# Front of a one-layer hybrid block: the first memory keys by plain fp32 products, and the loads in another order

## The chip, the core and the metric

The kernel runs on one core of a Trainium2 chip. The metric is device time in microseconds (us) of one execution. The core has a matrix engine (TensorE, "PE" in the profile, with its weight loads as "PEld"), a vector engine (VectorE, "DVE"), a scalar engine (ScalarE, "ACT"), GpSimd ("POOL") and SyncE ("SP"), which here only issues transfers. Each engine takes its instructions in order. Transfers from the chip's large memory are issued by SP, ACT or POOL; those of one issuer stand in one queue, and all share 16 DMA engines.

## The reference, cut to what matters

A layer works on 512 frames of 1024 channels (`x`) and on 256 memory tokens of 1024 channels (`mem`), in float32. `x` and `mem` are normalised, three branches attend, their gated sum goes through an output product, and a squared-ReLU MLP follows. This case concerns the first steps only:

```
u = rmsnorm(h, g_mix)                              # h = x at the start
mkv = rmsnorm(mem, g_mem) @ w_mem_kv               # 256 x 1024
mk, mv = split(mkv)                                # memory keys and values, 512 columns each
proj = u @ w_in                                    # every projection of the layer starts from u
```

The row factor of `rmsnorm(mem, g_mem)` is one number per memory token, so the kernel multiplies by `g_mem` first, forms the products, and applies that number later.

## The kernel before, in words

**Products in parts.** A float32 product is made of three fast products. Each operand is split: ACT casts it to the fast format (the high part, `hi`), DVE subtracts that from the original (the low part, `lo`). `mm3` (lines 154 to 157) then adds high by high, high by low and low by high into the same accumulator. Weights come as chunks of 128 partitions by 1024 numbers (512 KB); `chunk_list` gives their order. Chunks 0 to 3 are the four key blocks, 4 to 7 the values, 8 is a small gate chunk ("G"), and from 9 on come the projections of `u`.

**The front** (lines 251 to 363) runs once and before everything else. Its parts:

- Twelve products of zeros (line 279) keep TensorE busy until data arrive. A memset on GpSimd (line 276) makes their operand.
- ACT's queue brings the memory tokens in four pieces (`memr`, line 282). SP's queue brings the gains `cols`, then chunk 0 in quarters, chunk 1, two small pieces of the constants (`ident` and `ones`, 128 KB; `mhalf`, 4 KB), chunks 2 and 3, the four tiles of `x` (`xn`, line 300, 512 KB each), chunk 4, and the other constants (lines 302 to 304). `lead` (lines 258 to 269) issues such a chunk and splits it.
- ACT and DVE make the parts `mxh`, `mxl` of the memory tokens times `g_mem` (lines 288 and 289), one eighth at a time.
- Four key blocks (`mk_proj`) are 24 products of 128x256 each. For each contraction step `gT` issues all three products of `mm3`, so the low part of the weights is needed at the third product.
- `x_norm(t)` makes one tile of `x` ready: a sum of squares on ACT (line 327), two small steps on DVE and GpSimd (lines 214 and 215, the latter a power with `mhalf`), a scaling on DVE (line 329).
- `u_turn(k)` transposes one block of 128 channels of all four tiles on TensorE with the identity (line 341); ACT and DVE split the result into `uhi` and `ulo` (lines 342 and 343). The eight transposed blocks are taken in turn with the four value chunks: two blocks, one chunk (12 products of 128x512 for two token tiles), two blocks, one chunk, and so on. Here the second product already needs the low part of the weights.
- `g_proj` (lines 410 to 420) then projects `u` with chunk G, and the layer goes on with chunks 9, 10 and so forth.

**What sets the order.** TensorE's order is the order in which the code is written. The order on the other engines is planned: a simulated run at build time places each instruction by the time at which it is ready there; `issue_after` ties one instruction behind another. Buffers for raw chunks, high and low parts (`raw`, `hi`, `lo`) exist three times each; two more raw ones (`lead`) serve chunks 3 and 4. Four accumulator banks are for keys and projections, four for values and transposes. Each chunk split by `split_w` also counts towards `next_sum`, which from the twelfth on issues one weight-sum transfer per chunk on GpSimd's queue for the MLP.

The step that is split for the vector engine, as the front uses it:

```
raw, hi, lo = (t[:, sl] for t in pre[key])
nc.sync.dma_start(raw, wst[index[key]][:, sl])
cast = nc.scalar.copy(hi, raw).ins
nc.vector.tensor_tensor(lo, raw, f(hi), op=ALU.subtract)
```

Of the kernel before, what the change touches and what calls it, by code (L numbers as in the profile page):

```python
# [9 lines left out]
F32 = mybir.dt.float32  # L10
# [7 lines left out]
P = 128  # L18
# [46 lines left out]
def hybrid_block(ctx, tc, chunks, wst, memT, xN, cols, gffn, gfin, wup, cst, out):  # L65
# [26 lines left out]
        return ap.bitcast(F32)  # L92


    cst_s = cp.tile([P, 7 * P + 8], F32, name="cst_s")
    cols_s = cp.tile([P, 24], F32, name="cols_s")
    msk_s = cp.tile([P, 2, P], U8, name="msk_s")
    wup_s = cp.tile([P, 264], F32, name="wup_s")
    ident, ones, tri, mids = (cst_s[:, i * P:(i + 1) * P] for i in range(4))
    mhalf = cst_s[:, 6 * P:6 * P + 8]  # L100
    cmask = cst_s[:, 6 * P + 8:]
# [85 lines left out]
    def run(*gens):  # L187
        for g in gens:
            for _ in g:
                pass  # L190
# [60 lines left out]
    with pool("front") as fp:  # L251
# [4 lines left out]
        pre = {}  # L256

        def lead(key, n, i):
            if key not in pre:
                late = index[key] > 2  # L260
                pre[key] = [(fp if late else wp).tile([P, 1024], F32, tag="lead" if late else "raw", name=nm("raw"),
                                                      bufs=2 if late else 3)]
                pre[key] += [wp.tile([P, 1024], F32R, tag=g, name=nm(g)) for g in ("hi", "lo")]
            sl = slice(i * 1024 // n, (i + 1) * 1024 // n)
            raw, hi, lo = (t[:, sl] for t in pre[key])
            nc.sync.dma_start(raw, wst[index[key]][:, sl])
            cast = nc.scalar.copy(hi, raw).ins
            nc.vector.tensor_tensor(lo, raw, f(hi), op=ALU.subtract)
            return cast

        mxh = fp.tile([P, KT, M], F32R, name="mxh")
        mxl = fp.tile([P, KT, M], F32R, name="mxl")
        warm = fp.tile([P, 1], F32, name="warm")
        nc.vector.memset(warm, 0.0)
        wz = fp.tile([P, 512], BF16, name="wz")
        nc.gpsimd.memset(wz, 0.0)
        ps = at_()
        for _ in range(12):
            nc.tensor.matmul(ps, wz[:, :P], wz, start=True, stop=True)
        nc.sync.dma_start(cols_s, cols)  # L280
        for j in range(4):
            d = nc.scalar.dma_start(memr[:, 2 * j:2 * j + 2], memT[:, 2 * j:2 * j + 2]).ins
        with tc.issue_after(d):
            act = nc.scalar.activation(warm, warm, AF.Exp).ins
        for j in range(4):
            for k in (2 * j, 2 * j + 1):
                with tc.issue_after(act):
                    act = nc.scalar.mul(mxh[:, k, :], memr[:, k, :], gmem[:, k:k + 1]).ins
                nc.vector.scalar_tensor_tensor(mxl[:, k, :], memr[:, k, :], gmem[:, k:k + 1], f(mxh[:, k, :]),
                                               op0=ALU.mult, op1=ALU.subtract)  # L290
                if k == 2 * j:
                    with tc.issue_after(act):
                        act = lead(chunks[0], 4, j)
        lead(chunks[1], 1, 0)
        nc.sync.dma_start(cst_s[:, :2 * P], cst[:, :2 * P])
        nc.sync.dma_start(cst_s[:, 6 * P:6 * P + 8], cst[:, 6 * P:6 * P + 8])
        lead(chunks[2], 1, 0)
        lead(chunks[3], 1, 0)
        for t in range(NT):
            nc.sync.dma_start(xn[:, t, :], xN[t * P:(t + 1) * P, :])  # L300
        lead(chunks[4], 1, 0)
        nc.sync.dma_start(cst_s[:, 2 * P:6 * P], cst[:, 2 * P:6 * P])
# [13 lines left out]
        def mk_raw(h):  # L316
            return gkT[h // 2][:, (h % 2) * M:(h % 2) * M + M]
# [14 lines left out]
        def k_copies(after, hs):  # L332
            with tc.issue_after(after):
                for h in hs:
                    nc.scalar.copy(mk_raw(h), kps[h][:, :M])

        def u_turn(k):

            pt = at_()
            for t in range(NT):  # L340
                nc.tensor.transpose(pt[:, t * P:(t + 1) * P], xn[:, t, k * P:(k + 1) * P], ident)
            a = nc.scalar.mul(uhi[:, k, :], pt, gmix[:, k:k + 1]).ins
            return a, nc.vector.scalar_tensor_tensor(ulo[:, k, :], pt, gmix[:, k:k + 1], f(uhi[:, k, :]), op0=ALU.mult,
                                                  op1=ALU.subtract).ins
# [17 lines left out]
        run(mv)  # L362
        nc.vector.tensor_copy(msk_s.rearrange("p a b -> p (a b)"), cst_s[:, 4 * P:6 * P])
# [37 lines left out]
    with pool("fox") as xp:  # L401
# [8 lines left out]
        def g_proj():  # L410

            raw = load_w(("G",)).rearrange("p (k c) -> p k c", k=KT)
            w = wp.tile([P, 1024], F32R, tag="hi", name=nm("whi")).rearrange("p (k c) -> p k c", k=KT)
            nc.scalar.copy(w, raw)
            nc.vector.tensor_tensor(w[:, :, 64:], raw[:, :, 64:], f(w[:, :, 64:]), op=ALU.subtract)
            ps = mmt()
            for k in range(KT):
                nc.tensor.matmul(ps, w[:, k, :], uhi[:, k, :], start=k == 0, stop=False)
                nc.tensor.matmul(ps, w[:, k, :], ulo[:, k, :], start=False, stop=k == KT - 1)
            ga_evac(ps)  # L420
# [1005 lines left out]
def layout(inputs):  # L1426
# [52 lines left out]
    s = np.arange(P)[:, None]  # L1479
    t = np.arange(P)[None, :]  # L1480
    same = (s // 64) == (t // 64)
    cst = np.zeros((P, 7 * P + 8), np.float32)
    cst[:, 0:P] = np.eye(P)
    cst[:, P:2 * P] = 1.0
    cst[:, 2 * P:3 * P] = s <= t
    half = np.where(s < 64, -1.0 * (t < 63) * (s > t) + 1.0 * (t == 63), 1.0 * (s <= t) * (t > 63))
    cst[:, 3 * P:4 * P] = half / 16.0
    cst[:, 4 * P:5 * P] = s <= t
    cst[:, 5 * P:6 * P] = same & (s > t)
    cst[:, 6 * P:6 * P + 8] = -0.5  # L1490
    cst[:, 6 * P + 8:] = np.where(t > s, np.float32(NEG), 0.0)
# [29 lines left out]
```

## Time and profile before

| | before |
|---|---|
| median of 3 runs | 820.11 us (819.8 to 820.19) |
| the profiled execution, its own time | 822.02 us |
| its span, first to last instruction | 820.2 us |
| TensorE busy | 809.4 us, 99% of the span |
| VectorE / ScalarE / GpSimd busy | 591.4 / 439.1 / 103.7 us |
| mean granted TensorE clock | 0.995 |
| bytes moved | 155.60 MB, mean 190 GB/s |

The profiled execution takes 1.8 us more than its span and 1.9 us more than the median. Times in rows are us from the start of the span. A row of the timeline names its start, its duration, the engine, the line, the operation, what it writes and reads, the shape, and how many instructions were merged; in brackets stands the idle time of the engine before it and what ended it. A matrix product's duration overlaps the next one's, so its cost in a stream is the distance between starts. The table of stretches gives for each stretch the busy time of PE, PEld, DVE, ACT and POOL with the number of instructions, then the granted TensorE clock (1.00 is full), the busy share of the DMA engines and the bytes per time.

### The profile page before, as it was taken

The page shows a single profiled execution, that of the slowest core. Times are in us where ns is not written, and L with a number is a line of the kernel's source. Part 1 is how long each engine was busy: PE and PEld are TensorE (multiplying, and loading weights), DVE is VectorE, ACT ScalarE, POOL GpSimd, SP SyncE. Part 2 cuts the span into 40 slices and gives each one's busy share as a digit, 9 for nine tenths or more (in the row PEclk, how much of TensorE's full clock was granted, in tenths as well). Part 3 has the DMA queues.
Part 4 walks back from the last instruction along what each step waited for, and adds up shares of the span by engine and source line. Part 5 has one row for each costly group of instructions (what it writes and reads, how often), then busy time and mean ns, then how long its engine had stood idle before and what let it go on. Part 6 is the DMA issues. An engine that isn't in the chain of part 4 may idle for free.

```text
span 820.2 us, 12435 instructions
## 1 busy us (share of the span) xinstructions
PE 809.4 (99%) x4791; PEld 710.2 (87%) x4791; DVE 591.4 (72%) x910; ACT 439.1 (54%) x693; POOL 103.7 (13%) x125
## 2 busy tenths in 40 slices
PE   8999999999999999999999999999999999999996
PEld 6788888888888888999999889988998899889984
DVE  5745887538545676887577647897689778887896
ACT  7644756443345234434345436774576367647764
POOL 1001000011101121133232100011001100110011
PEclk9999999999999999999999999999999999999998
DMA  9534675688787884777665504978758866896643
GB/s 330 187 103 151 185 184 170 199 235 253 209 265 231 231 238 147 148 199 177 171 196 151 195 23 132 279 160 210 247 180 181 213 223 178 188 251 194 166 80 128
DMA packets 39180, 155.60 MB, mean 190 GB/s; under 512 B 4880, under 2 KB 5840, under 8 KB 37072
## 3 DMA queue, kind: packets, MB, share of 16 engines
q1 hardware_dynamic: 27712, 95.54, 33.2%
q0 software_dynamic: 9328, 54.01, 31.9%
q10 hardware_dynamic: 2080, 5.26, 2.0%
q8 instruction: 37, 0.61, 0.3%
q14 instruction: 23, 0.19, 0.1%
HBM read 152.65 MB, written 31.49 MB: 224 GB/s over the span
## 4 chain that ended last, share of the span: by engine, by line
PE 94%; DVE 2%; DMA 2%; issue 1%; ACT 0%; POOL 0%; ACTq 0%; POOLq 0%; DVEq 0%
PE mm L155 24%; PE mm L156 23%; PE mm L157 23%; PE a L156 5%; PE a L157 5%; PE a L155 5%; DMA xn<-in_xN_dram 1%; DMA memr<-in_memT_dram 1%; PE a L538 1%; PE a L576 1%; PE a L575 1%; DVE h L1181 1%; PE a L814 1%; DVE lo L1187 0%; PE a L825 0%
## 5 line engine op out<-in xcount | busy, mean ns | idle before, releaser
L146 DVE TENSOR_TENSOR wlo<-raw,whi 128x1024 fp32r<-128x1024 f32 x68 | 88.2, 1300 | 64.6 <-ACT whi L145 64.6
L155 PE MATMUL mm<-uhi,whi 128*128 128x512 f32 (+1 forms) x352 | 125.9, 358 | 0.0
L157 PE MATMUL mm<-uhi,wlo 128*128 128x512 f32 (+1 forms) x352 | 123.7, 351 | 0.0
L156 PE MATMUL mm<-ulo,whi 128*128 128x512 f32 (+1 forms) x352 | 123.5, 351 | 0.0
L145 ACT CAST whi<-raw 128x1024 fp32r<-128x1024 f32 x68 | 71.4, 1052 | 96.2 <-PE mm L156 54.0
L1185 ACT CAST hi<-raw 128x1024 fp32r<-128x1024 f32 x65 | 68.2, 1049 | 49.6 <-PE mm L156 32.7
L1187 DVE TENSOR_TENSOR lo<-raw,hi 128x1024 fp32r<-128x1024 f32 x65 | 79.5, 1223 | 17.7 <-ACT hi L1185 17.7
L155 PEld LDWEIGHTS mm<-uhi,whi 128*128 128x128 f32 x352 | 66.7, 189 | 9.9 <-issue 1.5
L157 PEld LDWEIGHTS mm<-uhi,wlo 128*128 128x128 f32 x352 | 66.6, 189 | 9.1
L156 PEld LDWEIGHTS mm<-ulo,whi 128*128 128x128 f32 x352 | 66.7, 189 | 8.1
L1185 ACT CAST hi<-b 128x1024 fp32r<-128x1024 f32 x40 | 41.9, 1048 | 42.0 <-PE mm L157 25.5
L157 PE MATMUL mm<-u2h,lo 128*128 128x256 f32 x224 | 63.4, 283 | 0.0
L156 PE MATMUL mm<-u2l,hi 128*128 128x256 f32 x224 | 63.4, 283 | 0.0
L155 PE MATMUL mm<-u2h,hi 128*128 128x256 f32 x224 | 63.4, 283 | 0.0
L1371 POOL DMA_DIRECT2D b<-in_wst_dram x32 | 27.3, 854 | 271.3 <-DVE lo L1187 206.4
L1187 DVE TENSOR_TENSOR lo<-b,hi 128x1024 fp32r<-128x1024 f32 x40 | 48.8, 1222 | 14.1 <-ACT hi L1185 14.0
L155 PE MATMUL mm<-hi,ch 128*128 128x512 f32 x136 | 52.9, 389 | 0.0
L156 PE MATMUL mm<-lo,ch 128*128 128x512 f32 x136 | 52.9, 389 | 0.0
L157 PE MATMUL mm<-hi,cl 128*128 128x512 f32 x136 | 52.9, 389 | 0.0
L155 PE MATMUL mm<-u2sh,hi 128*128 128x256 f32 x168 | 47.5, 283 | 0.0
L156 PE MATMUL mm<-u2sl,hi 128*128 128x256 f32 x168 | 47.5, 283 | 0.0
L157 PE MATMUL mm<-u2sh,lo 128*128 128x256 f32 x168 | 47.5, 283 | 0.0
(410 smaller groups left out, 2114.5 us busy)
## 6 DMA issues: line engine op xcount, KB each, us to landing
raw<-in_wst_dram SPq DMA_DIRECT2D x114, 512.0 KB
b<-in_wst_dram POOLq DMA_DIRECT2D x32, 512.0 KB, 5.4
raw<-T SPq DMA_DIRECT2D x28, 512.0 KB
T<-in_wst_dram POOLq DMA_DIRECT2D x12, 1024.0 KB, 9.5
b<-in_wst_dram SPq DMA_DIRECT2D x16, 512.0 KB
wb<-in_wst_dram POOLq DMA_DIRECT2D x15, 512.0 KB, 5.5
wb<-in_wst_dram SPq DMA_DIRECT2D x8, 512.0 KB
T<-in_wst_dram POOLq DMA_DIRECT2D x6, 512.0 KB, 5.1
```

The costliest lines, as they stand in the source:

```text
L145: cast = nc.scalar.copy(hi, raw)
L146: low_now[0] = nc.vector.tensor_tensor(lo, raw, f(hi), op=ALU.subtract).ins
L155: nc.tensor.matmul(ps, lh, rh, start=start, stop=False, skip_group_check=on)
L156: nc.tensor.matmul(ps, lh, rl, start=False, stop=False, skip_group_check=on)
L157: nc.tensor.matmul(ps, ll, rh, start=False, stop=stop, skip_group_check=on)
L538: nc.tensor.matmul(ps[e], q[a, sl], k[a, :w], start=p == 0, stop=p == 2)
L575: nc.tensor.matmul(po[:, q0:], vv, PTh[:, c0:c0 + w], start=n == 0, stop=False)
L576: nc.tensor.matmul(po[:, q0:], vv, PTl[:, c0:c0 + w], start=False, stop=n == 3)
L814: nc.tensor.matmul(ps[e][:, t, :], kk[half[e], sl], qq[half[e], sl], start=True, stop=True)
L1185: nc.scalar.copy(hi, raw)
L1187: nc.vector.tensor_tensor(lo, raw, f(hi), op=ALU.subtract)
L1371: nc.gpsimd.dma_start(to[i], wst[index["B", q, i, x]], accum_op=ALU.add)
```

## The change

Five things, all in the front.

1. The first key block is no longer split. Chunk 0 is multiplied by `g_mem` on DVE, in quarters, and TensorE forms 8 plain float32 products with the unsplit memory tokens instead of 24 products of parts. The casts and subtractions of chunk 0 are gone.
2. Chunk 1 comes in halves. Key blocks 1 to 3 issue all products with the high weights first and the 8 products with the low weights last.
3. Chunk 4 (first values) is loaded ahead of `x`, chunk 5 joins the chunks that the front loads by itself, and the first value chunk's 12 products stand ahead of the transposes. The transposes of blocks 0 and 1 take tiles 0 to 2 of both blocks first, then tile 3.
4. `ones` and `mhalf` are filled by GpSimd, the identity is loaded behind `x`, the other constants behind chunk 5.
5. Smaller things: nine products of zeros instead of twelve, their operand filled by DVE; the cast of chunk G is tied behind the split of the fourth transposed block; the cast of the masks (`msk_s`) is tied behind the last one.

```diff
-    cst_s = cp.tile([P, 7 * P + 8], F32, name="cst_s")
+    cst_s = cp.tile([P, 6 * P], F32, name="cst_s")
+    ones = cp.tile([P, P], F32, name="ones")
+    mhalf = cp.tile([P, 8], F32, name="mhalf")
...
         def lead(key, n, i):
             if key not in pre:
-                late = index[key] > 2
+                late = index[key] in (3, 4)
...
+        wz = fp.tile([P, 512], BF16, name="wz")
+        nc.vector.memset(wz, 0.0)
...
-        wz = fp.tile([P, 512], BF16, name="wz")
-        nc.gpsimd.memset(wz, 0.0)
         ps = at_()
-        for _ in range(12):
+        for _ in range(9):
             nc.tensor.matmul(ps, wz[:, :P], wz, start=True, stop=True)
...
+        plain = wp.tile([P, 1024], F32, tag="raw", name=nm("raw"))
+        keys = plain.rearrange("p (k c) -> p k c", k=KT)
         for j in range(4):
+            ks = slice(2 * j, 2 * j + 2)
+            nc.sync.dma_start(plain[:, 256 * j:256 * j + 256], wst[0][:, 256 * j:256 * j + 256])
             for k in (2 * j, 2 * j + 1):
                 with tc.issue_after(act):
                     act = nc.scalar.mul(mxh[:, k, :], memr[:, k, :], gmem[:, k:k + 1]).ins
                 nc.vector.scalar_tensor_tensor(mxl[:, k, :], memr[:, k, :], gmem[:, k:k + 1], f(mxh[:, k, :]),
                                                op0=ALU.mult, op1=ALU.subtract)
-                if k == 2 * j:
-                    with tc.issue_after(act):
-                        act = lead(chunks[0], 4, j)
-        lead(chunks[1], 1, 0)
-        nc.sync.dma_start(cst_s[:, :2 * P], cst[:, :2 * P])
-        nc.sync.dma_start(cst_s[:, 6 * P:6 * P + 8], cst[:, 6 * P:6 * P + 8])
-        lead(chunks[2], 1, 0)
-        lead(chunks[3], 1, 0)
+            g = gmem[:, ks].rearrange("p (k o) -> p k o", o=1).to_broadcast([P, 2, P])
+            nc.vector.tensor_tensor(keys[:, ks, :], keys[:, ks, :], g, op=ALU.mult)
+        for n in range(2):
+            lead(chunks[1], 2, n)
+        nc.gpsimd.memset(ones, 1.0)
+        nc.gpsimd.memset(mhalf, -0.5)
+        for n in (2, 3, 4):
+            lead(chunks[n], 1, 0)
         for t in range(NT):
             nc.sync.dma_start(xn[:, t, :], xN[t * P:(t + 1) * P, :])
-        lead(chunks[4], 1, 0)
-        nc.sync.dma_start(cst_s[:, 2 * P:6 * P], cst[:, 2 * P:6 * P])
+        nc.sync.dma_start(ident, cst[:, :P])
+        lead(chunks[5], 1, 0)
+        nc.sync.dma_start(cst_s[:, P:5 * P], cst[:, P:5 * P])
         nc.sync.dma_start(wup_s, wup)
-        nc.sync.dma_start(cmask, cst[:, 6 * P + 8:])
+        nc.sync.dma_start(cmask, cst[:, 5 * P:])
...
         def mk_proj(h):
-            run(gT(("T", "w_mem_kv", P * h), mxh, mxl, kps.append, n=M))
+            ps = mmt()[:, :M]
+            kps.append(ps)
+            if h == 0:
+                for k in range(KT):
+                    nc.tensor.matmul(ps, keys[:, k, :], memr[:, k, :], start=k == 0, stop=k == KT - 1)
+                return
+            hi, lo = (t.rearrange("p (k c) -> p k c", k=KT) for t in pre[chunks[h]][1:])
+            for k in range(KT):
+                nc.tensor.matmul(ps, hi[:, k, :], mxh[:, k, :], start=k == 0, stop=False)
+                nc.tensor.matmul(ps, hi[:, k, :], mxl[:, k, :], start=False, stop=False)
+            for k in range(KT):
+                nc.tensor.matmul(ps, lo[:, k, :], mxh[:, k, :], start=False, stop=k == KT - 1)
...
-        def u_turn(k):
-            pt = at_()
-            for t in range(NT):
+        def turn(pt, k, ts):
+            for t in ts:
                 nc.tensor.transpose(pt[:, t * P:(t + 1) * P], xn[:, t, k * P:(k + 1) * P], ident)
+        def u_split(pt, k):
             a = nc.scalar.mul(uhi[:, k, :], pt, gmix[:, k:k + 1]).ins
...
+        run(islice(mv, 4))
+        pts, u_mid = [at_() for _ in range(2)], None
+        for ts in (range(NT - 1), (NT - 1,)):
+            for k in range(2):
+                turn(pts[k], k, ts)
         for k in range(KT):
-            u_act, u_end = u_turn(k)
-            if k % 2:
+            if k > 1:
+                pts.append(at_())
+                turn(pts[k], k, range(NT))
+            u_act, u_end = u_split(pts[k], k)
+            u_mid = u_act if k == 3 else u_mid
+            if k in (1, 3, 5):
                 run(islice(mv, 4))
...
-        nc.vector.tensor_copy(msk_s.rearrange("p a b -> p (a b)"), cst_s[:, 4 * P:6 * P])
         get_w = get_plain
         with tc.issue_after(u_end):
+            nc.vector.tensor_copy(msk_s.rearrange("p a b -> p (a b)"), cst_s[:, 3 * P:5 * P])
...
-            nc.scalar.copy(w, raw)
+            with tc.issue_after(u_mid):
+                nc.scalar.copy(w, raw)
```

The host's layout of the constants follows the new tile: without the columns of ones and of -0.5.

More of the change, by code (lines that the diff above doesn't have):

```diff
@@ L98, in hybrid_block @@
     wup_s = cp.tile([P, 264], F32, name="wup_s")
-    ident, ones, tri, mids = (cst_s[:, i * P:(i + 1) * P] for i in range(4))
-    mhalf = cst_s[:, 6 * P:6 * P + 8]
-    cmask = cst_s[:, 6 * P + 8:]
+    ident, tri, mids = (cst_s[:, i * P:(i + 1) * P] for i in range(3))
+    cmask = cst_s[:, 5 * P:]
     gmix, gmem, ghead = cols_s[:, 0:8], cols_s[:, 8:16], cols_s[:, 16:20]
@@ L266, in lead @@
             nc.sync.dma_start(raw, wst[index[key]][:, sl])
-            cast = nc.scalar.copy(hi, raw).ins
+            nc.scalar.copy(hi, raw)
             nc.vector.tensor_tensor(lo, raw, f(hi), op=ALU.subtract)
-            return cast
         mxh = fp.tile([P, KT, M], F32R, name="mxh")
         mxl = fp.tile([P, KT, M], F32R, name="mxl")
+        wz = fp.tile([P, 512], BF16, name="wz")
+        nc.vector.memset(wz, 0.0)
         warm = fp.tile([P, 1], F32, name="warm")
         nc.vector.memset(warm, 0.0)
-        wz = fp.tile([P, 512], BF16, name="wz")
-        nc.gpsimd.memset(wz, 0.0)
         ps = at_()
-        for _ in range(12):
+        for _ in range(9):
             nc.tensor.matmul(ps, wz[:, :P], wz, start=True, stop=True)
@@ L334, in k_copies @@
                 for h in hs:
-                    nc.scalar.copy(mk_raw(h), kps[h][:, :M])
-        def u_turn(k):
-            pt = at_()
-            for t in range(NT):
+                    nc.scalar.copy(mk_raw(h), kps[h])
+        def turn(pt, k, ts):
+            for t in ts:
                 nc.tensor.transpose(pt[:, t * P:(t + 1) * P], xn[:, t, k * P:(k + 1) * P], ident)
+        def u_split(pt, k):
             a = nc.scalar.mul(uhi[:, k, :], pt, gmix[:, k:k + 1]).ins
@@ L1481, in layout @@
     same = (s // 64) == (t // 64)
-    cst = np.zeros((P, 7 * P + 8), np.float32)
+    cst = np.zeros((P, 6 * P), np.float32)
     cst[:, 0:P] = np.eye(P)
-    cst[:, P:2 * P] = 1.0
-    cst[:, 2 * P:3 * P] = s <= t
+    cst[:, P:2 * P] = s <= t
     half = np.where(s < 64, -1.0 * (t < 63) * (s > t) + 1.0 * (t == 63), 1.0 * (s <= t) * (t > 63))
[L1487 to L1491, printed above, removed]
+    cst[:, 2 * P:3 * P] = half / 16.0
+    cst[:, 3 * P:4 * P] = s <= t
+    cst[:, 4 * P:5 * P] = same & (s > t)
+    cst[:, 5 * P:] = np.where(t > s, np.float32(NEG), 0.0)
     arrays = {
```

## The prediction

> **What bounds the kernel now.** I read the page first, then the chain of waits, then TensorE's waits alone.
>
> ```profile
> span 820.2 us, 12435 instructions
> PE 809.4 (99%) x4791; PEld 710.2 (87%) x4791; DVE 591.4 (72%) x910; ACT 439.1 (54%) x693; POOL 103.7 (13%) x125
> PE 94%; DVE 2%; DMA 2%; issue 1%; ACT 0%; POOL 0%; ACTq 0%; POOLq 0%; DVEq 0%
> ```
>
> ```profile
> PE a L279 <- POOL wz L276: 1.3, 1, 1.3
> PE a L341 <- DVE xn L329: 1.2, 1, 1.2
> PE mm L157 <- DVE lo L268: 0.8, 1, 0.8
> PE a L156 <- DVE lo L268: 0.3, 1, 0.3
> ```
>
> TensorE bounds the whole; the four waits shown are its only ones, all in the front. So a microsecond by which the front hands over earlier should come off the end, if nothing behind needs more than that. The hand-over is the first product of `g_proj` (L418). The stretch before it, in the timeline:
>
> ```profile
> 20.33 0.28 PE L157 MATMUL mm<-mxh,lo 128*128 128x256 f32 x1
> 20.45 0.74 PE L341 MATMUL a<-cst_s,xn 128*128 128x128 f32 x3
> 22.41 0.77 PE L341 MATMUL a<-cst_s,xn 128*128 128x128 f32 x5 [1.22 <-DVE xn L329]
> 22.93 0.48 PE L155 MATMUL a<-hi,mxh 128*128 128x512 f32 x1
> 23.74 0.58 PE L156 MATMUL a<-lo,mxh 128*128 128x512 f32 x1 [0.34 <-DVE lo L268]
> ...
> 27.96 1.04 PE L341 MATMUL a<-cst_s,xn 128*128 128x128 f32 x8
> 28.76 0.48 PE L155 MATMUL a<-whi,mxh 128*128 128x512 f32 x1
> ...
> 31.62 1.03 PE L341 MATMUL a<-cst_s,xn 128*128 128x128 f32 x8
> ...
> 35.23 1.03 PE L341 MATMUL a<-cst_s,xn 128*128 128x128 f32 x8
> ...
> 38.84 0.39 PE L418 MATMUL mm<-uhi,whi 128*128 128x512 f32 x1
> ```
>
> The keys end at 20.45. Three of the eight first transposes run; the other five wait for the last tile of `x` until 22.41. Then come four periods of one value chunk and two transposed blocks. Later ones take 3.66 and 3.61 us (27.96, 31.62, 35.23); the first chunk alone takes 22.93 to 27.96, 5.03 us. The table of stretches says why:
>
> ```profile
> 12.00:18.00 6.00, 6.00 (x50) 6.00 (x51) 3.42 (x5) 4.78 (x7) 0.64 (x2) 1.00 1.02 414
> 20.60:24.02 3.42, 1.84 (x11) 1.10 (x9) 2.69 (x6) 2.20 (x5) 0.55 (x1) 1.00 0.82 323
> 24.02:27.44 3.42, 3.42 (x9) 2.66 (x9) 3.35 (x4) 1.90 (x3) 0.00 (x0) 0.50 0.12 28
> ```
>
> After a stretch in which TensorE was busy 1.84 of 3.42 us, it has half its clock (0.50) for 3.42 us. The wait for `x` costs twice. A product of 128x256 costs 6.00/50 = 0.12 us in the first row, and the DMA engines are full there at 414 GB/s: `x` comes as early as the bytes ahead of it allow.
>
> **The change part by part.** The rows of ACT, DVE and SP on which the terms rest:
>
> ```profile
> 13.78 1.05 ACT L267 CAST hi<-raw 128x1024 fp32r<-128x1024 f32 x1 [0.26 <-DMA raw<-in_wst_dram]
> 17.63 1.06 ACT L327 ACTIVATE xsq<-xn 128x1024 f32<-128x1024 f32 x1 [0.18 <-DMA xn<-in_xN_dram]
> 18.92 1.06 ACT L327 ACTIVATE xsq<-xn 128x1024 f32<-128x1024 f32 x1
> 20.50 1.06 ACT L267 CAST hi<-raw 128x1024 fp32r<-128x1024 f32 x1
> 22.77 1.26 ACT L342 ACTIVATE uhi<-a,cols_s 128x512 fp32r<-128x512 f32 x2 [1.22 <-PE a L341]
> ```
>
> ```profile
> 5.44 0.42 DVE L268 TENSOR_TENSOR lo<-raw,hi 128x256 fp32r<-128x256 f32 x1 [0.18 <-ACT hi L267]
> 9.73 0.48 DVE L289 SCALAR_TENSOR_TENSOR mxl<-memr,cols_s,mxh 128x256 fp32r<-128x256 f32 x1
> 10.67 1.22 DVE L268 TENSOR_TENSOR lo<-raw,hi 128x1024 fp32r<-128x1024 f32 x1 [0.46 <-ACT hi L267]
> 21.59 0.76 DVE L329 TENSOR_SCALAR xn<-xn,rr 128x1024 f32<-128x1024 f32 x1 [0.73 <-POOL rr L215]
> 22.26 0.29 DVE L363 CAST msk_s<-cst_s 128x256 uint8<-128x256 f32 x1
> 22.46 1.22 DVE L268 TENSOR_TENSOR lo<-raw,hi 128x1024 fp32r<-128x1024 f32 x1
> 23.60 1.41 DVE L343 SCALAR_TENSOR_TENSOR ulo<-a,cols_s,uhi 128x512 fp32r<-128x512 f32 x2
> ```
>
> ```profile
> 1.32 5.30 PE L279 MATMUL a<-wz 128*128 128x512 bf16 x12 [1.32 <-POOL wz L276]
> 11.95 0.38 PE L157 MATMUL mm<-mxh,lo 128*128 128x256 f32 x1 [0.76 <-DVE lo L268]
> 53.51 1.78 PE a L434 x8
> ```
>
> *Key block 0.* Eight plain products replace 24. The nearest row is L434 (chain of waits), plain products too: four of 264 columns, each in two instructions, 1.78/4 = 0.445 us each, so 0.43 for 256 columns and 3.45 for eight, against 24 x 0.12 = 2.9 now. This 0.55 is hidden, because the block waits for its data. On DVE four subtractions of 0.42 become four multiplications of the same shape; the gain's repeated operand has no row, so I take 0.42, with the 0.48 of the three-operand form as upper end and a half of 0.42 as lower. DVE finishes its eighths at 9.73 + 0.48 = 10.2; the last two plain products need 0.86 more, so the block ends by 11.1. ACT loses four casts of 0.4, covered likewise.
>
> *Blocks 1 to 3.* Low parts now come after 16 products (1.9 us), so the wait before 11.95 goes; halving chunk 1 starts its split earlier, worth nothing behind that. 72 x 0.12 = 8.6 us: the keys end at 19.7, 0.75 earlier than now.
>
> *The first value chunk ahead.* The next chunk's 12 products run from 28.76 to 31.62, 2.86 us or 0.24 each at full clock; taken from 19.7 they end at 22.56. Chunk 3 lands by 13.78 today; without the 132 KB ahead of it (0.3) and with 512 KB more (1.3) chunk 4 lands by 14.8, and a cast of 1.05 and a subtraction of 1.22 make its low part ready by 17.1: no wait. Six transposes at 0.10 (five from 22.41 to 22.93) follow to 23.2.
>
> *`x` comes later.* Moved ahead of it on SP's queue: chunk 4, 512 KB; taken away: 128 + 4 KB of constants. 380 KB are 389,000 bytes, at 414 GB/s 0.94 us. Bounds: 0, if the delay between bytes and landing absorbs it, and 1.3, if the constants gave nothing back. SP itself issues two transfers more (chunk 4, the second half of chunk 1) and two less (the constants) ahead of `x`; what it waits for is covered by the full DMA engines (the squares at 17.63 and 18.92 are 1.3 us apart, the time of 512 KB at that rate). The chain of square, power and scaling moves along: the last tile is ready at 21.59 + 0.76 + 0.94 = 23.3, while TensorE's path is ready at 23.2. Two transposes remain; with the 0.06 between the scaling and TensorE's start today they end at 23.57.
>
> *Chunk 5 behind `x`.* The identity (64 KB) and chunk 5 bring 590,000 bytes, 1.4 us at that rate, behind the last tile (18.92 + 0.94): near 21.3. Chunk 5 waits on SP for the buffer of the plain keys, free at 11.1, long before the DMA engines are through with `x`; behind it wait the other constants, which nothing reads before L434 at 53, and chunk 6. Its low part (1.22) is then next on DVE behind the scaling, as chunk 4's is now at 22.46: 23.3 to 24.52. The second value product therefore starts at 24.58 (0.06 later) instead of 23.81, a wait of 0.77, more than the 0.34 now. Bounds 0 and 1.2. The mask cast (0.29) has left this place; it now runs behind the last `ulo`, where nothing waits for it soon.
>
> *From there.* Eleven products at 0.24 end at 27.2. Two periods of 3.66 and 3.61 and two transposed blocks of 0.80 (27.96 to 28.76) give 27.2 + 7.27 + 0.80 = 35.27 for the hand-over, against 38.84: **3.6 us earlier**. The last chunk no longer covers the split of blocks 6 and 7, but the first twelve products of `g_proj`, of the same shape, do (2.9 us against 1.26 on ACT and 1.41 on DVE).
>
> *At no cost:* `ones` and `mhalf` on GpSimd, which waits for the first power until `x` is in; the identity, right behind `x`; chunk G's cast behind the fourth split, a period ahead of its need; weight sums one chunk later. *Nine zero products* at 5.30/12 = 0.44 end near 5.2, and a short gap follows until the first multiplied quarter. If that keeps the half clock, the plain products cost 0.86 each instead of 0.43; the bounds are 0 and 1.7 us for half the block. A block ending 0.9 late has TensorE at the last tile 0.8 late, which the 0.77 of wait for chunk 5's low part takes up; so I take nothing.
>
> So the span goes from 820.2 to 816.6, the profiled execution's own time from 822.02 to 818.4, and the median, which is 1.9 below that, from 820.11 to **816.5**.
>
> **The rivals.** *The half clock comes anyway.* After the change the stretch up to 24.02 holds products to 22.56, transposes to 23.2, and 0.45 more: 3.0 of 3.42 us. The stretch that led to the half clock had 1.84. Between them lies a case that kept full clock: the wait of 0.76 before the product at 11.95 leaves about 2.7 of 3.42. [...] Price: from 24.58 to 27.44 half of the work is lost, 1.4 us, so 817.9. [...]
>
> *VectorE or ScalarE becomes the bound.* Between 23.3 and the hand-over the same work is now done in 12 us instead of 16. DVE, by the rows above: three low parts 3.7, eight `ulo` at 0.7 5.6, half of chunk G 0.6, 9.9 in all; ACT: eight `uhi` at 0.63 5.0, casts of chunks 6, 7, G and the next 4.2, two squares of `memr`, of the shape of `xsq`, 2.1, and two copies: 11.3 and more. It fits only just. One instruction of 1.2 in the wrong place is a wait: 817.7; two, 818.9.
>
> *Slower: chunk 5 in front of `x` on ACT.* In the code its cast now stands ahead of the squares. If the plan keeps that order, the four squares wait for chunk 5 (21.3) and its cast: from 22.4 on at 1.3 each, and 3.4 from the last one's start to its scaling's end (18.92 to 22.35), the last tile is ready at 22.4 + 3.9 + 3.4 = 29.7, 6.4 us later than forecast, and the half clock returns (1.7): 816.5 + 6.4 + 1.7 = 824.6. It decides from a delay of 3.6 on. Against it: chunk 4's cast stands ahead of the squares in the code today and ran at 20.50, behind all of them.
>
> *The chunk ahead gains nothing*, because work behind the hand-over was waiting for something else: no wait of TensorE after 24 us speaks for that. 820.1.
>
> **How the numbers follow.** Forecast 0.62, with its own range 815.2 (no wait for chunk 5's low part and a little less delay of `x`) to 817.2; half clock 0.13; DVE or ACT bound 0.11; slower by ACT's order 0.10; nothing gained 0.04. About 0.2%, 1.6 us, is what a measurement here can tell from no change. The first two cases and most of the third are faster by more: 0.83. Within: 0.06. Slower: 0.11. The range takes in the third case with two misplaced steps: 815.0 to 819.0.
>
> **What would show it.** L418's first start near 35.3, the last `xn` scaling ending near 23.3, a values product between the last key product and the first transpose, full clock from 24 to 27.4, and a wait of about 0.8 for chunk 5's low part. Wrong would be: squares behind chunk 5's cast, a second half-clock stretch, or new waits of TensorE behind the front.

## The result

| | before | after |
|---|---|---|
| median of 22 executions each | 820.20 us (819.4 to 823.59) | 818.77 us (818.04 to 819.89) |
| the profiled execution, its own time | 822.02 us | 819.0 us |
| its span | 820.2 us | 817.2 us |
| mean granted TensorE clock in it | 0.995 | 0.999 |

The ratio is 0.9982, 95% interval 0.9976 to 0.9988: the change takes off 1.43 us, and between 1.0 and 2.0. The forecast was 816.5, a gain of 3.6. The two profiled executions differ by 3.0 us; this gap between 3.0 and 1.43 is what the experiments had to explain.

The page of the profile after, its span, busy times and shares of the chain:

```profile
span 817.2 us, 12414 instructions
PE 806.5 (99%) x4780; PEld 707.8 (87%) x4780; DVE 593.7 (73%) x912; ACT 438.4 (54%) x690; POOL 103.6 (13%) x126
PE 92%; DMA 3%; DVE 2%; issue 1%; ACT 1%; POOL 0%; POOLq 0%; ACTq 0%; SPq 0%; DVEq 0%
```

TensorE's waits after (who waits, for what, us in total, times, longest):

```profile
PE a L280 <- DVE warm L277: 1.2, 1, 1.2
PE a L157 <- DVE lo L270: 0.7, 1, 0.7
PE a L357 <- DVE xn L347: 0.6, 1, 0.6
PE mm L333 <- DVE raw L297: 0.5, 1, 0.5
PE mm L158 <- DVE wlo L147: 0.4, 1, 0.4
```

The wait of 0.8 for a low part of the keys is gone, the one for `x` has shrunk from 1.2 to 0.6, the one for the low part of a value chunk has grown from 0.3 to 0.7. The last line is new in kind: it lies at 370 us, far behind the front.

TensorE's timeline after, the second part of key block 0 and then the work around `x`:

```profile
7.14 3.14 PE L333 MATMUL mm<-memr,raw 128*128 128x256 f32 x12 [0.45 <-DVE raw L297]
9.93 0.47 PE L337 MATMUL mm<-mxh,hi 128*128 128x256 f32 x1
...
17.79 1.12 PE L340 MATMUL mm<-mxh,lo 128*128 128x256 f32 x8
18.75 0.40 PE L156 MATMUL a<-hi,mxh 128*128 128x512 f32 x1
...
21.50 0.81 PE L357 MATMUL a<-cst_s,xn 128*128 128x128 f32 x6
22.89 0.44 PE L357 MATMUL a<-cst_s,xn 128*128 128x128 f32 x2 [0.58 <-DVE xn L347]
23.08 0.48 PE L156 MATMUL a<-hi,mxh 128*128 128x512 f32 x1
...
24.29 0.50 PE L157 MATMUL a<-lo,mxh 128*128 128x512 f32 x1 [0.72 <-DVE lo L270]
...
26.92 1.04 PE L357 MATMUL a<-cst_s,xn 128*128 128x128 f32 x8
...
30.55 1.03 PE L357 MATMUL a<-cst_s,xn 128*128 128x128 f32 x8
...
34.16 1.03 PE L357 MATMUL a<-cst_s,xn 128*128 128x128 f32 x8
...
34.95 0.48 PE L446 MATMUL mm<-uhi,whi 128*128 128x512 f32 x1
```

The value chunk stands between keys (end 18.75) and transposes (21.50), six transposes run and two wait for the last tile, and the hand-over is at 34.95. The table of stretches after (busy PE, PEld, DVE, ACT, POOL, then the granted clock, the DMA share and GB/s):

```profile
4.80:8.20 3.40, 2.90 (x9) 1.58 (x8) 2.74 (x8) 1.96 (x5) 0.00 (x0) 1.00 1.05 368
8.20:11.70 3.50, 3.49 (x23) 3.20 (x23) 3.27 (x8) 2.25 (x5) 0.00 (x0) 1.00 0.97 341
20.60:24.02 3.42, 2.39 (x14) 1.62 (x12) 2.52 (x4) 2.28 (x5) 0.55 (x1) 1.00 0.94 356
24.02:27.44 3.42, 3.15 (x16) 2.65 (x17) 3.38 (x5) 2.50 (x3) 0.00 (x0) 1.00 0.48 162
```

No half clock. So the front does nearly what was forecast, and yet the time falls by less than half of it. Two places can hold the rest: the starting point (38.84), and what follows the front (817.2 − 34.95 = 782.25, against 820.2 − 38.84 = 781.36 before).

### The profile page after: what moved, and what is told of

The parts are those of the page before. It is cut to its first block, busy times and chain, and to the rows that moved or that the text cites. A ratio compares the mean times of both kernels' runs of the same rounds, so it can differ in the third digit from the quotient of the medians.

```text
span 817.2 us, 12414 instructions
## 1 busy us (share of the span) xinstructions
PE 806.5 (99%) x4780; PEld 707.8 (87%) x4780; DVE 593.7 (73%) x912; ACT 438.4 (54%) x690; POOL 103.6 (13%) x126
## 4 chain that ended last, share of the span: by engine, by line
PE 92%; DMA 3%; DVE 2%; issue 1%; ACT 1%; POOL 0%; POOLq 0%; ACTq 0%; SPq 0%; DVEq 0%
PE mm L156 23%; PE mm L158 23%; PE mm L157 23%; PE a L157 5%; PE a L156 5%; PE a L158 5%; DMA raw<-in_wst_dram 2%; DMA wb<-in_wst_dram 1%; PE a L566 1%; DMA memr<-in_memT_dram 1%; PE a L604 1%; PE a L603 1%; DVE h L1209 1%; PE a L842 1%; DVE wlo L147 1%
```

## The experiments

Names: an execution's *rest* is its span less its hand-over. Each kernel's median stands beside that of the kernel before in the same session.

**1. The kernel before again** (E1, no edit) and **filled** (E2): is the half clock what most executions have?

> The kernel before, unchanged, with the span and clock of every execution. Theory A (the half-clock stretch of 3.4 us after the wait for x stands in the profiled execution but not in most): the executions fall into two kinds, those with a mean granted clock near 0.995 and those with 0.997 or more, and the first take 1.5 to 2 us longer; the median, near 820.2, belongs to the second kind. Rival B (the half clock is in every execution, and the front's 3.9 us are given back behind the hand-over): all clocks are near 0.995 and the time does not go with the clock.

```
# e2, ahead of k_copies(x_act, (0, 1)):
+ ps = at_()
+ for _ in range(5):
+     nc.tensor.matmul(ps, wz[:, :P], wz, start=True, stop=True)
```

> The kernel before with five products of zeros (1.15 us at full clock) between the last key product and the transposes, while TensorE waits for the last tile of x. Nothing that the kernel needs moves. Both theories: no half clock between 20 and 30 us, first values chunk in about 2.9 us plus a wait of about 0.3, so L418 (here L421) starts near 36.9 instead of 38.84. Theory A: the median gains only what the share of half-clock executions is worth, 0 to 0.7 us (819.5 to 820.2). Rival B: it gains the whole 1.9 us (818.3).

The stretches of E1:

```profile
20.60:24.02 3.42, 2.31 (x13) 1.64 (x12) 3.14 (x5) 2.20 (x4) 0.25 (x1) 1.00 0.79 315
24.02:27.44 3.42, 3.42 (x20) 2.89 (x19) 3.14 (x4) 2.77 (x5) 0.00 (x0) 1.00 0.29 71
```

and of its timeline, the scaling of the last tile of `x`, the transposes that wait for it, and the hand-over:

```profile
20.88 0.75 DVE L329 TENSOR_SCALAR xn<-xn,rr 128x1024 f32<-128x1024 f32 x1 [0.73 <-POOL rr L215]
21.69 0.77 PE L341 MATMUL a<-cst_s,xn 128*128 128x128 f32 x5 [0.76 <-DVE xn L329]
...
36.49 0.39 PE L418 MATMUL mm<-uhi,whi 128*128 128x512 f32 x1
```

The same program, and the clock stays whole: the last tile is ready at 20.88 + 0.75 = 21.63 instead of 22.35, TensorE waits 0.76 instead of 1.22 and is busy 2.31 instead of 1.84 of the 3.42 us. The hand-over comes 2.35 earlier, the span is 2.2 shorter (818.0). The execution that the prediction read was of a rarer kind. Of 116 executions of this kernel in the sessions of these experiments, 6 have its mean clock of 0.995, 822.34 in the median (one of them took only 820.38); the other 110 have 0.996 to 0.999 and a median near 820.1. The mean clock is a blunt sign: the six profiles before, E1, E5, E6, E7 and after also have half clock at their end (0.50 behind 815.92 before, behind 815.89 in E1, behind 814.85 after), which takes 0.001 to 0.003 off the mean, as much as the 3.41 us in the front, so 0.996 and 0.997 alone don't exclude a half clock there. But the 45 executions at 0.997 have a median of 820.10, those at 0.998 and 0.999 of 820.13 and 820.00, so few of the 45 can have it. E2's five zero products lie in the wait; its median is 820.11 against 820.03, ratio 1.0003 [0.9994, 1.0012], and none of its 11 executions is at 0.995. There was nothing to gain in the median.

**2. `x` later in the kernel before** (E8): does a longer wait bring the half clock to all?

```
+ nc.sync.dma_start(cst_s[:, 2 * P:6 * P], cst[:, 2 * P:6 * P])   # now ahead of x
  for t in range(NT): ...
  lead(chunks[4], 1, 0)
- nc.sync.dma_start(cst_s[:, 2 * P:6 * P], cst[:, 2 * P:6 * P])
```

> The kernel before with one transfer moved: 256 KB of constants ahead of x instead of behind chunk 4, so x is 0.65 us later and nothing else changes. If the length of the wait decides on the half clock: the wait grows from 0.76 to about 1.4, most executions show a mean clock of 0.995, and the median rises by 0.65 plus about 1.7, to 822.3. If the half clock falls by chance: the median rises by the 0.65 alone, to 820.7.

The stretch in E8, and the wait for `x` in its timeline:

```profile
20.60:24.02 3.42, 2.07 (x13) 1.37 (x12) 2.69 (x5) 2.20 (x4) 0.55 (x1) 1.00 0.85 337
```

```profile
22.64 0.76 PE L341 MATMUL a<-cst_s,xn 128*128 128x128 f32 x5 [1.21 <-DVE xn L329]
```

Not so. The wait grew by 0.45, to the length it had in the first profile (1.21 and 1.22), the hand-over (37.23) came 0.74 later than in E1 and 0.23 later than in E10 (below), yet the clock stayed whole (1.00 in 24.02 to 27.44); 1 of 11 executions is at 0.995 and the median is 820.59 against 820.41, ratio 1.0007 [0.9997, 1.0016]. The length of this wait alone does not decide.

The stretch 20.60 to 24.02 doesn't mean the same in every profile, though. The granted clock of the first profile falls to 0.50 at 24.02, is 1.00 again from 27.44 and falls again at 815.92. It is 0.70 over 24.02 to 24.03, 0.65 over 27.43 to 27.44 and 0.90 over 815.90 to 815.92, which puts the changes at 24.024, 27.437 and 815.916: the first two lie 3.413 us apart, the last two 788.479, 231 times that. So in this profile the changes lie on a raster. That the other executions have one of the same step, placed by the change near their end (815.89 in E1), is an assumption of the author's and is not shown. The stretches so placed that hold the wait for `x`, before, in E1 and in E8:

```profile
20.61:24.02 3.41, 1.83 (x11) 1.10 (x9) 2.68 (x6) 2.19 (x4) 0.55 (x1) 1.00 0.82 323
20.58:24.00 3.42, 2.31 (x14) 1.64 (x12) 3.12 (x5) 2.20 (x4) 0.27 (x1) 1.00 0.81 319
19.66:23.07 3.41, 2.20 (x18) 1.81 (x17) 2.06 (x4) 2.19 (x6) 1.10 (x2) 1.00 1.02 400
```

In the first profile the stretch holds the wait for `x` and the one of 0.34 for a low part at 23.74; in E8, as placed, it ends at 23.07 and holds the wait for `x` alone. Where the raster happened to lie is thus, if the assumption holds, a rival to the busy time and to the wait, and no run held it fixed.

**3. The keys alone** (E3): plain key block 0, chunk 1 in halves and the low products last, nothing moved.

```
+ plain = wp.tile([P, 1024], F32, tag="raw", name=nm("raw"))   # loaded in quarters, times g on DVE
- act = lead(chunks[0], 4, j)
- lead(chunks[1], 1, 0)
+ for n in range(2):
+     lead(chunks[1], 2, n)
  # mk_proj as in the changed kernel
```

> The kernel before with the plain key block 0, chunk 1 in halves and the high-first order of blocks 1 to 3, loads and the order of transposes and values as before. My working says that it is worth nothing: the keys end near 19.7 instead of 20.45, the transposes still wait for the last tile until 22.4, the hand-over stays where it was. The idle time grows by 0.75, so the half clock should come no less often: median 820.2 to 821. Rival (the key products set the time): 819.5 or less.

TensorE's waits and the stretches of E3:

```profile
PE a L357 <- DVE ms L214: 1.4, 2, 1.2
PE a L279 <- POOL wz L276: 1.3, 1, 1.3
PE a L357 <- DVE xn L345: 1.2, 1, 1.2
PE a L156 <- DVE lo L268: 0.3, 1, 0.3
```

```profile
20.60:24.02 3.42, 1.33 (x7) 0.82 (x7) 2.69 (x6) 2.30 (x5) 0.55 (x1) 1.00 0.98 387
24.02:27.44 3.42, 3.36 (x8) 2.67 (x9) 3.42 (x5) 2.23 (x3) 0.00 (x0) 0.54 0.08 31
```

Slower: 822.34 against 820.03, ratio 1.0026 [1.0016, 1.0036], and 6 of 8 executions are at 0.995. Keys that end earlier only make TensorE idle longer before `x`, 2.6 us in three waits, and now the half clock is the usual case. The two executions at 0.997 and 0.998 took 821.83 and 821.07, which points to a loss besides the clock; the last tile was ready at 22.69 in this profile, 1.06 later than in E1.

**4. The order alone** (E4): chunk 4 ahead of `x`, its products ahead of the transposes, keys as before.

```
+ lead(chunks[4], 1, 0)          # ahead of the x loop instead of behind it
+ run(islice(mv, 4))             # then three tiles of blocks 0 and 1, then the last
- if k % 2:
+ if k in (1, 3, 5):
```

> The kernel before with chunk 4 ahead of x, the first value chunk ahead of the transposes, and the transposes of blocks 0 and 1 in two goes; keys and constants as before, and no tie for the cast of chunk G. x comes 1.3 us later, last tile ready near 23.6, no half clock, hand-over near 35.6 if no cast stands in the way; the median then gains 1.0 to 1.3 us against before (819 to 819.2) by theory A, 2.9 to 3.2 by rival B. If the cast of chunk G ahead of the splits of blocks 2 and 3 holds these up, a wait of up to 1 us shows at the transposes and the gain is smaller by that.

Of E4's timeline, the cast of chunk 4 on ACT:

```profile
15.56 1.05 ACT L267 CAST hi<-raw 128x1024 fp32r<-128x1024 f32 x1 [0.86 <-PE mm L156]
```

The hand-over is at 36.40 and the median 819.46 against 820.03, 0.57 less, ratio 0.9995 [0.9986, 1.0003]: by itself not to be told from nothing. The cast waits 0.86 for TensorE, which still reads the buffer of the high parts of chunk 1; the squares stand behind it, and the last tile is ready at 24.13, 2.5 later than in E1, of which the 512 KB more ahead of `x`, by the prediction's 1.3, explain about half. In the changed kernel, whose plain block takes no such buffer, this cast starts at 14.23 behind its load, and the last tile is ready 1.3 (22.83) or 0.9 (E5, 23.24) earlier than here: the order seems to gain from the plain keys, though the constants have moved there too.

**5. The constants alone** (E12): `ones` and `mhalf` by memset, identity and the rest behind `x`.

```
- nc.sync.dma_start(cst_s[:, :2 * P], cst[:, :2 * P])
- nc.sync.dma_start(cst_s[:, 6 * P:6 * P + 8], cst[:, 6 * P:6 * P + 8])
+ nc.gpsimd.memset(ones, 1.0)
+ nc.gpsimd.memset(mhalf, -0.5)
  for t in range(NT): ...
+ nc.sync.dma_start(ident, cst[:, :P])
```

> The kernel before with the constants' part of the change alone: ones and -0.5 filled by GpSimd, identity behind x, the smaller constant tile. In the front x comes 132 KB or 0.3 us earlier, so the wait for the last tile shrinks by up to 0.3 and the hand-over should be near 36.2 to 36.7, the median 0.3 below before, with a half clock at most as often. For the load near 360 us: 6 us or more if the smaller constants or the two transfers less are what lengthens it in all six profiles of kernels with the whole change (5.95 to 7.64 against 5.38 to 5.59 in seven others); 5.4 to 5.6 if it is something else.

Hand-over 36.04, median 819.71 against 820.10, 0.39 less, ratio 0.9995 [0.9986, 1.0004]. `x` was ready at 20.91, 0.72 before E1, but the keys' low part costs 0.8 as before and the first cast 0.7.

**6. The changed kernel with key block 0 in parts** (E7): what do the plain products bring?

```
- plain = wp.tile([P, 1024], F32, tag="raw", name=nm("raw"))   # and its load and multiplication
+ act = lead(chunks[0], 4, j)
  # in mk_proj: block 0 as the others, 24 products
```

> The changed kernel with key block 0 in parts again (cast, subtraction, 24 products), everything else as changed. If the plain products bring nothing of their own, because TensorE reaches the last tile of x ahead of it anyway (values ended at 21.5, transposes would at 22.1, tile ready at 22.8): the keys end up to 0.7 later, the hand-over moves by less than 0.2, median 818.7 to 819. If the plain products carry the gain: 819.3 or more.

E7's stretches, to be held against the first two rows of the changed kernel above:

```profile
4.80:8.20 3.40, 2.69 (x9) 1.41 (x8) 3.02 (x7) 2.99 (x9) 0.00 (x0) 1.00 1.04 379
8.20:11.70 3.50, 3.44 (x13) 3.00 (x14) 3.32 (x7) 2.80 (x8) 0.00 (x0) 0.52 1.03 362
```

Median 819.63 against 820.41, ratio 0.9988 [0.9979, 0.9996]; the changed kernel in the same session (E5) has 819.16. Behind 8.33 TensorE has half its clock here (0.52 over 8.20 to 11.70), and 13 instead of 23 products run; with the plain products it is whole (1.00). The keys end later, the hand-over is at 35.26 against 35.09. By the median the plain products bring some 0.5 us, which is the rival of the expectation; by the hand-over 0.17, which is its first case; and the two intervals overlap. The half clock does not explain the 0.5: three executions of E7 without it (mean clock 0.999) took 819.63 to 819.80, the four at 0.996 only 818.57 to 819.17.

Nor does busy time explain why the clock fell. The 3.41 us that led to the half clock in E7, and stretches that did not, in E5 and in E6 (below), both with plain products and placed by the assumption above:

```profile
4.92:8.33 3.41, 2.64 (x10) 1.48 (x9) 3.10 (x8) 3.00 (x8) 0.00 (x0) 1.00 1.06 386
5.40:8.81 3.41, 2.37 (x9) 1.47 (x10) 2.76 (x8) 2.42 (x7) 0.00 (x0) 1.00 1.16 369
4.27:7.69 3.42, 2.31 (x10) 1.30 (x9) 2.34 (x6) 2.62 (x6) 0.00 (x0) 1.00 1.00 349
```

TensorE was busier where it lost the clock, 2.64 us against 2.37 and 2.31. The profile counts a product that costs 0.12 us in a stream with 0.38 where it stands alone, as many do in E7, so busy time is no measure of the work done.

**7. The changed kernel again** (E5, no edit), with **the old count of weight sums** (E9), and the kernel before with **a later count** (E10): where do 0.7 to 0.9 us go behind the front?

> The changed kernel, unchanged. By the theory that the half clock belongs to a wait for x of more than about 1.2 us, which the change has taken away: no execution with a mean clock of 0.995, median 818.6 to 818.9, hand-over near 35. The wait of TensorE at 370 us (0.45 for the low part of a block whose load took 7.4 us) was chance: it is not there again, and this profile's span is then 0.5 or more shorter than 817.2. Rival (the change has shifted the transfers so that this wait is its price): it is there again, at the same product.

```
- chunk_n, cast_now, low_now = [0], ...
+ chunk_n, cast_now, low_now = [1], ...    # e9, in the changed kernel; [-1] in e10, in the kernel before
```

> The changed kernel with the count of split chunks starting at 1, so that the weight sums on GpSimd's queue come with the same chunks as before. If the later sums cause the long load near 360 us (7.4 and 7.6 us from issue to cast in the two profiles of the changed kernel, 5.4 to 5.6 in six profiles of kernels with the old count): the load takes 5.4 to 5.6 here, TensorE has no wait at 370, and the median is about 0.7 below the changed kernel's 818.8 to 819.2. If something else in the change causes it: load of 6 or more, and no change of the median.

> The kernel before with the count starting at -1, so that the sums come one chunk later, as in the changed kernel, and nothing else. If the later sums are the cause: the load near 362 us takes 6 or more, with a wait of TensorE of up to 0.6 behind it, and the median rises by 0 to 0.7 above before. If not: load of 5.4 to 5.6, no wait, median as before.

A load of a block `wb` on GpSimd's queue, from its issue to its cast, in the changed kernel:

```profile
360.26 0.88 POOL L974 DMA_DIRECT2D wb<-in_wst_dram  x1
367.66 1.05 ACT L146 CAST whi<-wb 128x1024 fp32r<-128x1024 f32 x1 [4.99 <-DMA wb<-in_wst_dram]
```

in E1:

```profile
361.47 0.86 POOL L946 DMA_DIRECT2D wb<-in_wst_dram  x1
367.01 1.05 ACT L145 CAST whi<-wb 128x1024 fp32r<-128x1024 f32 x1 [3.14 <-DMA wb<-in_wst_dram]
```

and in E9:

```profile
360.90 0.87 POOL L974 DMA_DIRECT2D wb<-in_wst_dram  x1
367.20 1.05 ACT L146 CAST whi<-wb 128x1024 fp32r<-128x1024 f32 x1 [3.91 <-PE a L158]
```

5.54 us from issue to cast became 7.40. The issue comes 1.2 earlier and the cast 0.65 later, TensorE waits 0.45 at 370.02 for the low part that follows (the product starts 0.73 behind the one before it instead of 0.12), and the rest grows from 781.51 to 782.25. It is no chance of one execution: E5 has 7.64, a wait of 0.6 at the same place, a rest of 782.41, and a median of 819.16 against 820.41 (0.9984 [0.9975, 0.9993]). The theory that the weight sums, issued one chunk later, take the load's place fell: with the old count issue to cast still takes 6.30, though the cast then waits for a buffer that TensorE reads and TensorE itself waits for nothing there (rest 781.52), and the median is 818.97 against 819.88 (0.9987 [0.9978, 0.9996]), no other gain than without, given the intervals; the later count in the kernel before leaves it at 5.38 and the median where it was (0.9998 [0.9989, 1.0007]). Keys, order and constants alone leave it at 5.59, 5.44 and 5.48. Only kernels with nearly the whole change lengthen it (5.95 to 7.64 in six profiles). They are also the six that hand over earliest, at 34.30 to 35.68 against 36.04 and later in the others; whether the code or the earlier front lengthens it, no run separates. What does it stays open.

**8. High products first in the value chunks** (E6), and with the old count (E11): does the wait of 0.7 for chunk 5's low part come off the end?

```
+ for n, (l, r) in enumerate(((mxh, whi), (mxl, whi), (mxh, wlo))):   # per chunk: low weights last
+     for t in range(2):
+         for kk in range(2):
+             nc.tensor.matmul(pss[t], l[:, k, t * P:(t + 1) * P], r[:, kk, :], ...)
```

> The changed kernel with the twelve products of each value chunk in another order: the eight with the high weights first, the four with the low weights last. The wait of 0.72 for chunk 5's low part should go (it is then needed 1.9 us after the high part instead of 0.23): hand-over 0.7 earlier than the changed kernel's, median 818.0 to 818.2. Rival (what is won in the front is not passed on to the end): 818.7.

> Both in one: the high-first order of the value products and the old count of sums, on the changed kernel. If both are worth what the theory says: hand-over near 34.3, no wait near 370, median 817.7 to 818.2, below both the changed kernel and the high-first one (818.4).

E6's waits:

```profile
PE a L280 <- DVE warm L277: 1.2, 1, 1.2
PE mm L333 <- DVE raw L297: 1.1, 2, 0.8
PE a L357 <- DVE xn L347: 0.6, 1, 0.6
```

The wait for the low part is gone, and the hand-over is at 34.30, 0.65 and 0.79 before the two profiles of the changed kernel. The median is 818.40 against 820.41, ratio 0.9978 [0.9969, 0.9987], the lowest of all and 0.76 below E5 beside it. E11, the same with the old count, hands over 0.54 before E9 and has 818.83 against 819.88 (0.9985 [0.9977, 0.9994]), 0.14 below E9 beside it, and missed its forecast. E6's profiled execution is the fastest of its eleven (817.61), so its rest of 781.50 does not show that the loss at 370 us is gone for good. A better version than both kernels is likely, but these runs do not separate it from the changed kernel.

All profiles in one table; "ready" is the end of the last scaling of `x`, "busy" that of TensorE in 20.60 to 24.02, "clock" the granted one in 24.02 to 27.44 (the stretches ahead of and with the half clock of the first profile):

| | hand-over | rest | ready | busy | clock |
|---|---|---|---|---|---|
| before | 38.84 | 781.36 | 22.35 | 1.84 | 0.50 |
| E1 before again | 36.49 | 781.51 | 21.63 | 2.31 | 1.00 |
| E2 filled | 36.83 | 781.47 | 21.95 | 3.02 | 1.00 |
| E10 later count | 37.00 | 781.40 | 22.11 | 2.29 | 1.00 |
| E8 `x` late | 37.23 | 781.37 | 22.58 | 2.07 | 1.00 |
| E3 keys alone | 39.13 | 781.47 | 22.69 | 1.33 | 0.54 |
| E4 order alone | 36.40 | 781.60 | 24.13 | 3.42 | 1.00 |
| E12 constants alone | 36.04 | 781.56 | 20.91 | 3.08 | 1.00 |
| after | 34.95 | 782.25 | 22.83 | 2.39 | 1.00 |
| E5 after again | 35.09 | 782.41 | 23.24 | 2.80 | 1.00 |
| E7 block 0 in parts | 35.26 | 781.54 | 22.67 | 3.42 | 1.00 |
| E9 old count | 35.68 | 781.52 | 23.82 | 2.66 | 1.00 |
| E6 high first | 34.30 | 781.50 | 23.12 | 2.83 | 1.00 |
| E11 high first, old count | 35.14 | 781.66 | 23.84 | 2.65 | 1.00 |

## Why the prediction was right in direction and wrong in size

**The step that failed** is the last of the sum: "and the median, which is 1.9 below that, from 820.11 to 816.5". It carries the profiled execution's 1.9 over the median along as if both kernels had it. It was the price of a rare execution: of the half clock, about 1.6 at the hand-over against E8, where `x` was as late, and of an `x` that came 0.7 later than in E1. The forecast took this off the median, which hardly has it. The changed kernel's profiled execution took 819.0, 0.23 above its median instead of 1.9. So of the 2.27 us by which 816.5 was missed, 1.7 are this step; the other 0.6 is the difference between 819.0 and the forecast 818.4, a hand-over 0.3 earlier and a rest 0.9 longer. The sign was in the view: a mean clock of 0.995, and a time 1.9 above a median whose three runs lie within 0.4. From the usual hand-over of 36.49 (E1) or 37.00 (E10) the changed kernel's 34.95 and 35.09 are 1.4 to 2.05 earlier; the forecast's 3.6 counted from the rare one's 38.84.

That 818.77 lies inside the range of 815.0 to 819.0 is luck: it lies above the 817.2 of the forecast's own range, and the part above was there for VectorE or ScalarE as the bound, which they did not become.

**What followed the front.** "If nothing behind needs more than that" held for every profile but the two of the changed kernel itself: the rest is 781.36 to 781.66 in the others, 782.25 and 782.41 there. So 0.6 to 1.05 us are lost again. Product by product E5 is 0.04 behind E1 from the hand-over up to that place, and 0.9 behind it from the wait at 370 us to the end, so the loss lies there. The profiles' spans then differ by 0.85 (818.0 and 818.4 against 817.2 and 817.5), the medians by 1.43, whose interval reaches from 1.0; how much of the loss the usual execution has is not settled.

**The steps inside the front.**
- Key block 0 ends at 9.93; forecast by 11.1.
- The keys end at 18.75; forecast 19.7. The wait for their low part went, as forecast.
- The first value chunk waits for nothing and ends at 21.50, 2.75 behind its start; forecast 22.56, with 2.86.
- The last tile is ready at 22.83 and 23.24; forecast 23.3. Against E1's 21.63 it is 1.2 and 1.6 later, against the 22.35 of the first profile 0.5 and 0.9. With TensorE early, the two last transposes wait 0.58 instead of hardly at all. The prediction let only the loads set this time. In the changed kernel the four scalings start at 17.50, 18.99, 20.54 and 22.08, 1.5 apart, though the squares start 1.3 apart (15.42, 16.71, 18.05, 19.39): VectorE waits 0.7 for GpSimd's power ahead of each scaling, and the small step of the next tile stands behind that scaling on VectorE. The last tile's small step starts at 21.21, 0.66 behind the end of its sum of squares:

```profile
20.36 0.18 ACT L345 ACTIVATION_READ_ACCUMULATOR xsq<-xn 128x1 f32 x1
20.54 0.76 DVE L347 TENSOR_SCALAR xn<-xn,rr 128x1024 f32<-128x1024 f32 x1 [0.73 <-POOL rr L216]
21.21 0.15 DVE L215 TENSOR_SCALAR ms<-ssx 128x1 f32<-128x1 f32 x1
22.08 0.75 DVE L347 TENSOR_SCALAR xn<-xn,rr 128x1024 f32<-128x1024 f32 x1 [0.73 <-POOL rr L216]
```

- The wait for chunk 5's low part is 0.72; forecast 0.77. It costs what it lasts: E6 takes it away and gains 0.65 to 0.79 at the hand-over.
- The two periods are 3.63 and 3.61; forecast 3.66 and 3.61.
- The hand-over is 34.95; forecast 35.27.

"I take nothing" for the nine zero products was right here; with block 0 in parts the half clock did come (E7, 0.52 over 8.20 to 11.70). "No wait" for the value chunk seems to need the plain block, which leaves the buffers of the parts free: in E4 the chunk's cast waited for one.

**The rivals.** The half clock after the change did not come: 2.39 of 3.42 us, and full clock (1.00). Elsewhere in these runs it came behind stretches of 3.41 or 3.42 us with 1.33 (E3), 1.83 (before) and 2.64 us (E7) of busy time. VectorE and ScalarE did not become the bound; the only wait of TensorE behind the front is the one at 370 us, and the row of the cast there names a load. Chunk 5's cast did not come in front of the squares, but at 21.93 behind the last of them. That nothing is gained was excluded by the interval.

## What to carry to other kernels

Before a profiled execution is used as the starting point, hold its own time and granted clock against the other executions; where it stands out by more than they scatter, find what it has and they have not, and price the change without it. Work brought forward pays only if something fills the place up to the next late arrival: the keys alone were 2.3 us slower, the whole change, with the value chunk in the gap and the loads reordered, 1.4 us faster. And a gain is only earned at the end of the span: compare the rest behind the hand-over too.

## What the runs showed of the hardware

- In the first profile the granted clock fell to 0.50 at 24.02, was 1.00 from 27.44 on and fell again at 815.92; the changes lie 3.413 and 788.479 us apart, 1 and 231 steps of 3.413. In E3 it was 0.54 over 24.02 to 27.44, in E7 0.52 over 8.20 to 11.70. Near the end it fell at 815.89 in E1, at 814.85 after the change and at 813.88 in E7.
- The half clock followed stretches of 3.41 or 3.42 us with 1.33 (E3, 20.60 to 24.02), 1.83 (before, 20.61 to 24.02) and 2.64 us (E7, 4.92 to 8.33) of busy time, with single waits of at most 1.22, and in the first profile the hand-over came 1.6 later than in E8, where `x` was as late, and 2.35 later than in E1. It did not follow 2.07 (E8) and 2.31 us (E1) in 20.60 to 24.02, nor, in stretches placed by the author's assumption, 2.20 (E8), 2.31 (E1, E6) or 2.37 (E5). So the profile's busy time is not its measure; what is, is not shown.
- The time at which `x` is ready varies between executions of one program: 21.63, 21.95, 22.11 and 22.35 in four profiles with the same order of loads up to `x`. It does not decide on the half clock alone: with 22.35 it came, with 22.58 in E8 it did not.
- Plain float32 products of 128x256 cost up to 0.47 each in a stream: in the changed kernel twelve instructions, two per product, took from 7.14 to 9.93, and the prediction's 0.43, from L434, was near.
- One load on GpSimd's queue near 360 us took 5.4 to 5.6 us from issue to cast in the eight profiles without the whole change, and 5.95 to 7.64 in the six with it or nearly so, more than 320 us behind the last hand-over of the front, before which the code differs. The six are also the six earliest hand-overs. The cause is open.
